# Attention logits from a pair of PSUM banks, and 512-column weight tiles in a two-block network on one Trainium2 core

## The chip, the cores and the metric

One core of one Trainium2 chip runs the whole kernel. The metric is the device time of one execution in microseconds. Three timed executions of the kernel before took 1380.38, 1381.72 and 1386.56 us, median 1381.72 us.

## The reference

Two networks run one after the other on 256 tokens of 1024 channels. Each has two layers. A layer of the first one normalises the stream, modulates it by the vector `c`, multiplies it by one wide matrix, runs three mixers of 8 heads of 64 channels, gates them and merges them:

```python
u = rms_norm(x, norm_g) * (1 + scale[:, None]) + shift[:, None]
z = u @ w_in
ya = dsa_attention(...)              # top-k by an index score, then softmax
yb = swa_sinks_attention(...)        # a window of 128 keys, with sinks
yc = stick_breaking_attention(...)
merged = sigmoid(ma) * (ya @ w_br_a) + sigmoid(mb) * (yb @ w_br_b) + sigmoid(mc) * (yc @ w_br_c)
x = x + gate[:, None] * (merged @ w_out)
```

A layer of the second network works on two streams of 256 tokens, a context and x. Its four mixers are HGRN2 (a gated linear scan, from context to x), grouped attention with normed queries and keys, differential attention (two softmax maps over 32 channels each; the second times lambda is subtracted), and window attention with a sink; 4 heads each. For x the attentions see 512 keys (context and x), for the context 256.

## The kernel before, in words

The streams are kept channel-major, as [128 channels, 8, 256 tokens]. **Large products.** Operands are float32 values that are split exactly into two float32r parts, high and low, and each product takes three matmuls for each 128 input channels: high by high, high by low, low by high. A weight tile has 256 columns. `raw` (L212) loads half of it, 512 rows and so 512 KB, by one DMA from SP's queue; `wtile` (L223) has `split` (L110) copy it to `wh` on ScalarE (L111) and subtract it to `wl` on VectorE (L112). There are three buffers for raw weights and four each for `wh` and `wl`. `proj_tok` (L248) makes a token-major result [128 tokens, 2 token tiles, up to 256 columns] in one PSUM bank: 128x128 pieces of the stream are loaded as TensorE's stationary operand, and the weights move past them, 256 columns a matmul; one token tile is computed to the end, then the other. `proj_ch` (L259) makes a channel-major result, with pieces of the weights stationary and 256 tokens moving. Token-major results that need rotary embedding go through `rope` on VectorE (L359, L370) and are transposed on TensorE by `tok_to_ch` (`T`, L108). All other matmuls are recorded under `mm`, L104. The index scores of block 1 have 324 columns, made as tiles of 256 and 68.

**PSUM.** The eight banks are four pools: `pj` 3 (projections), `lg` 2 (logits), `tr` 2 (transposes), `py` 1 (outputs of attention).

**Attention.** `probs` (L389) takes one bank of `lg`, holding the logits of one head (512 keys), two heads (256) or four (128). VectorE reduces the maximum from it (L397), ScalarE takes the exponentials and their row sums (L402); the bank is free when these are done. `weights_t` (L598) scales by the reciprocal (L610), transposes by TensorE, and copies the result to SBUF (L617); in `diff`, `p_times_v` (L405) does the last two (L412), behind the subtraction of the two maps (L931 to L933). Heads lie two to a 128-channel tile: even heads use rows 0 to 63 of TensorE's array, odd heads rows 64 to 127. In `gqa` (L883), `causal_softmax` (L620) and the index scores (L492) the bank of one row group is written with both its heads, or its one, then that of the other group. `diff` (L911) multiplies the queries by a mask to `qz` (L921), so that a product over all 128 rows sees only the 32 channels of one map. The levels of the scan `gla` (L753), and its first level `small`, issue all products of one row group to one bank, then those of the other group to the other.

**Order.** The program text gives the work; the Tile framework's scheduler then lays it out as one fixed order for each engine, by simulated times. Independent work (the gates' projections, the modulation products `ada`) is so placed between the steps of the softmax. At run time each engine takes its instructions in that order and waits at semaphores. The loop of `gqa` over the banks of logits reads (L890):

```python
for hs in ([[0, 2], [1, 3]] if nh == 2 else [[h] for h in range(4)]):
...
    e = self.probs(hs, L, logits, nm, ss, nsink)
    pt = self.weights_t(e, hs, L, nm, ss, sink)
```

Of the kernel before, what the change touches and what calls it, by code (L numbers as in the profile page):

```python
# [27 lines left out]
def _ap(t, base, dims):  # L28
# [5 lines left out]
       ("cs32", (2, 2, 32)), ("dmask", (4,)))  # L34
# [24 lines left out]
class Net:  # L59
    """Residual streams are kept channel-major, [128 channels, 8, 256 tokens].  Operands of the large products are  # L60
    float32 values split exactly into two float32r parts (high, low); a product takes high*high + high*low + low*high."""

    BUFS = {"th": 3, "pe": 3, "ro": 2, "rt2": 1, "pt": 3, "kc": 1, "gc": 1, "rstd": 1, "score": 1, "cs": 1, "rc": 1, "g1": 1, "g2": 1, "g4": 1}

    def __init__(self, ctx, tc, I):
# [11 lines left out]
        self.lg = pool("lg", 2, space=ps)  # L77
# [7 lines left out]
    # ---------------------------------------------------------------- tiles  # L85
# [9 lines left out]

    def halves(self, name, tags):
        """a [128, 8, 256] tile in two pieces"""
        return Halves([self.K(name, [128, 4, 256], tag=t) for t in tags])
# [15 lines left out]
    # ------------------------------------------------------------ constants  # L114
    def load_consts(self):
# [6 lines left out]
        self.mhalf = C.tile([128, 8], F32, name="mhalf")  # L122
# [20 lines left out]
    def more_consts(self):  # L143
# [34 lines left out]
        # -lambda of the differential attention, per layer  # L178
# [13 lines left out]
        # forget gate lower bounds -> f = A + B * tanh(z / 2)  # L192
# [18 lines left out]
    # -------------------------------------------------------------- weights  # L211
    def raw(self, ap, k0, c0, n, spare=False):  # L212
        """rows k0*128..(k0+4)*128, columns c0..c0+n"""
        if spare and self.spare:
            w = self.K("wsp", [128, 4, 256], tag=self.spare[self.nspare % len(self.spare)])
            self.nspare += 1
        else:
            w = self.wr.tile([128, 4, 256], F32, name="wr", tag="wr")
        self.nc.sync.dma_start(out=w[:, :, :n], in_=ap[k0 * 128:k0 * 128 + 512, c0:c0 + n].rearrange(  # L219
            "(k p) n -> p k n", p=128))  # L220
        return w

    def wtile(self, ap, c0, n=256, kt=8, pre=None):  # L223
        """columns c0..c0+n of ap [kt*128, N], split: w[part](k) -> [128, n]"""
        hs, ls = [], []
        for k in range(0, kt, 4):
# [1155 lines left out]
```

## Time and profile before

| | |
|---|---|
| time, median of 3 | 1381.72 us |
| profiled execution: span from first to last instruction | 1377.4 us |
| TensorE (PE) busy | 1330.4 us, 97% |
| weight loads of TensorE (PEld) busy | 1164.2 us, 85% |
| VectorE (DVE) busy | 844.3 us, 61% |
| ScalarE (ACT) busy | 655.1 us, 48% |
| mean granted TensorE clock | 0.986 |
| HBM traffic | 205.07 MB, mean 149 GB/s |

The profile comes from one execution with its own time. The page gives its span, 1377.4 us, 4.3 us below the median of the three timed runs; that difference is what lies around the span. In rows, names stand as out<-in: `ps` is any PSUM tile, `ps<-wh,uh` a product with `wh` moving past a piece of `uh`, or the other way round. A float32 matmul of the program shows as two records (two passes), so counts of attention matmuls in the trace are twice those of the program. Ends of matmuls are modelled, so the distance between starts is what tells how long one holds the array.

### The profile page before, as it was taken

Reading aid. Unit: us, or ns where it says so; the run is one execution under the profiler, and the core shown is the slowest. Engines: PE = TensorE matmul, PEld = TensorE weight load, DVE = VectorE, ACT = ScalarE, POOL = GpSimd, SP = SyncE. Lnnn points to the kernel's source line nnn. Section 1 sums busy time; section 2 is a strip of 40 time slices with the busy share of each in tenths; the row PEclk is TensorE's granted clock in tenths of the full one; section 3 lists DMA queues with packets and bytes.
Section 4 is the critical chain, followed back from the end, with each engine's and each line's share of the span. In section 5 each row is a group of like instructions: output and inputs, shape, how many; then the busy total and the mean of one; then the engine's idle time right before and its main releaser. Section 6 shows DMA issues by size and latency. Waiting matters only on the chain.

```text
span 1377.4 us, 27990 instructions
## 1 busy us (share of the span) xinstructions
PE 1330.4 (97%) x11682; PEld 1164.2 (85%) x11682; DVE 844.3 (61%) x1744; ACT 655.1 (48%) x1178; POOL 25.4 (2%) x23
## 2 busy tenths in 40 slices
PE   5999999999999999999998999999999998999996
PEld 2998987899889898789998989977877788997774
DVE  3795454655559544565576366756577777775764
ACT  3455555544444545654443233346455546534652
POOL 0000000000000000000000000000000000000000
PEclk9899999999999999999999999999999999999998
DMA  9754746568746474547764442322143355522111
GB/s 330 216 151 131 232 142 190 158 204 266 227 124 184 123 212 141 153 138 220 211 214 153 135 142 63 109 93 77 52 139 118 107 154 159 175 81 62 62 62 46
DMA packets 199214, 205.07 MB, mean 149 GB/s; under 512 B 8368, under 2 KB 197424, under 8 KB 198448
## 3 DMA queue, kind: packets, MB, share of 16 engines
q1 hardware_dynamic: 199088, 203.28, 48.3%
q8 instruction: 92, 1.51, 0.4%
q14 instruction: 34, 0.28, 0.1%
HBM read 199.06 MB, written 4.19 MB: 148 GB/s over the span
## 4 chain that ended last, share of the span: by engine, by line
PE 82%; DMA 6%; DVE 4%; issue 4%; ACT 2%; SPq 1%; POOL 0%; POOLq 0%; ACTq 0%; DVEq 0%
PE ps L104 77%; PE ps L108 5%; DMA wr<-w_in 4%; DMA wsp<-w_ada 2%; DVE wl L112 2%; ACT wh L111 1%; SPq L219 1%; DMA wr<-w_out 0%; DMA cT<-ctx 0%; DVE KTc L829 0%; DVE af L439 0%; ACT Xx L1305 0%; ACT pe L402 0%; ACT L566 0%; DVE QTc L827 0%
## 5 line engine op out<-in xcount | busy, mean ns | idle before, releaser
L112 DVE TENSOR_TENSOR wl<-wr,wh 128x1024 fp32r<-128x1024 f32 (+1 forms) x270 | 328.4, 1217 | 258.3 <-ACT wh L111 255.8
L111 ACT ACTIVATE wh<-wr 128x1024 fp32r<-128x1024 f32 (+1 forms) x270 | 284.6, 1055 | 378.2 <-PE ps L104 255.2
L104 PE MATMUL ps<-uh,wh 128*128 128x256 f32 x704 | 202.2, 287 | 2.4 <-ACT thm L566 2.4
L104 PE MATMUL ps<-ul,wh 128*128 128x256 f32 x704 | 200.9, 285 | 0.0
L104 PE MATMUL ps<-uh,wl 128*128 128x256 f32 x704 | 200.8, 285 | 0.0
L104 PEld LDWEIGHTS ps<-uh,wh 128*128 128x128 f32 x704 | 132.7, 188 | 8.2 <-issue 4.4
L104 PEld LDWEIGHTS ps<-ul,wh 128*128 128x128 f32 x704 | 132.8, 189 | 1.9 <-issue 1.7
L104 PEld LDWEIGHTS ps<-uh,wl 128*128 128x128 f32 x704 | 132.7, 188 | 1.9 <-issue 1.6
L104 PE MATMUL ps<-wh,uh 128*128 128x256 f32 (+1 forms) x416 | 120.2, 291 | 2.0 <-ACT uh L440 1.2
L104 PE MATMUL ps<-wl,uh 128*128 128x256 f32 (+1 forms) x416 | 119.9, 289 | 1.0 <-DVE wl L112 1.0
L104 PE MATMUL ps<-wh,ul 128*128 128x256 f32 (+1 forms) x416 | 120.0, 289 | 0.1
L402 ACT ACTIVATE pe<-ps,nm 128x512 f32<-128x512 f32 (+2 forms) x160 | 84.9, 539 | 54.4 <-DVE nm L397 41.1
L397 DVE TENSOR_REDUCE nm<-ps 128x1 f32<-128x512 f32 (+2 forms) x104 | 71.1, 687 | 42.2 <-PE ps L104 42.0
L104 PEld LDWEIGHTS ps<-wh,uh 128*128 128x128 f32 x416 | 81.2, 196 | 4.1 <-ACT uh L440 1.4
L104 PEld LDWEIGHTS ps<-wl,uh 128*128 128x128 f32 x416 | 81.3, 196 | 1.8 <-DVE wl L112 1.3
L104 PEld LDWEIGHTS ps<-wh,ul 128*128 128x128 f32 x416 | 81.5, 196 | 1.2 <-DVE ul L441 0.9
L104 PE MATMUL ps<-wh,hxh 128*128 128x256 f32 x256 | 72.4, 283 | 0.0
L104 PE MATMUL ps<-wh,hxl 128*128 128x256 f32 x256 | 72.1, 281 | 0.0
L104 PE MATMUL ps<-wl,hxh 128*128 128x256 f32 x256 | 72.0, 281 | 0.0
L104 PE MATMUL ps<-hxh,wh 128*128 128x256 f32 x224 | 64.9, 294 | 4.2 <-ACT hxh L440 4.2
L104 PE MATMUL ps<-hxl,wh 128*128 128x256 f32 x224 | 64.6, 290 | 2.7 <-DVE hxl L441 2.7
L104 PE MATMUL ps<-hxh,wl 128*128 128x256 f32 x224 | 64.6, 290 | 0.6 <-DVE wl L112 0.6
(351 smaller groups left out, 3150.7 us busy)
## 6 DMA issues: line engine op xcount, KB each, us to landing
wr<-w_in SPq DMA_DIRECT2D x204, 512.0 KB, 4.0
wsp<-w_ada SPq DMA_DIRECT2D x68, 512.0 KB, 5.7
wr<-w_out SPq DMA_DIRECT2D x40, 512.0 KB, 3.7
wr<-w_ada SPq DMA_DIRECT2D x28, 512.0 KB, 3.9
wr<-w_br_a SPq DMA_DIRECT2D x8, 512.0 KB, 3.9
wr<-w_br_c SPq DMA_DIRECT2D x8, 512.0 KB, 4.6
wr<-w_br_b SPq DMA_DIRECT2D x8, 512.0 KB, 4.6
Xx<-resx SPq DMA_DIRECT2D x2, 1024.0 KB, 4.7
```

The costliest lines, as they stand in the source:

```text
L104: self.nc.tensor.matmul(o, l, r, start=start, stop=stop, skip_group_check=True)
L108: self.nc.tensor.transpose(o, i, self.ident[:n, :n])
L111: self.nc.scalar.activation(h, x, AF.Copy)
L112: self.nc.vector.tensor_tensor(l, x, h, op=OP.subtract)
L219: self.nc.sync.dma_start(out=w[:, :, :n], in_=ap[k0 * 128:k0 * 128 + 512, c0:c0 + n].rearrange("(k p) n -> p k n", p=128))
L397: nc.vector.tensor_reduce(nmx, p, axis=AX.X, op=OP.max, negate=True)
L402: nc.scalar.activation(e[:, j, :], p[:, j, :], AF.Exp, bias=nm[:, h:h + 1], accum_out=ss[:, h:h + 1])
```

## The change

**Logits.** The pool `lg` holds one tile of two banks, `pp`, in place of two single banks. The new `banks` issues the logits alternately: a product of row group 0 to the first bank, one of row group 1 to the second, and so on. This is used in `causal_softmax` and `gqa`, and written out for the index scores and in `gla`. The tile is one buffer: the next pair of logits waits until the last reader of both banks is done. `diff` drops the mask product; the queries and keys of its two maps are now operands of 32 rows, one bank for each map, with 512 keys as with 256. With 256 keys, the maximum is now taken by two reductions of 256 columns in place of one of 512.

**Projections.** A weight tile of more than 256 columns is loaded in chunks of two 128-row groups of 512 columns: the same 512 KB, in rows of 2 KB in place of 1 KB. The products go through a chunk for both token tiles before the next chunk; a wide token-major projection has two banks of `pj`, one for each token tile. The 324 columns of the index scores are one tile. In block 1, `idx`, `aq`, `ak`, `av`, `cv` and `bq` are wide; in block 2 queries, keys and values of mixer B, queries and keys of C, values of C with queries of D. `rope` runs for each token tile by itself (`rope_1`). `proj_ch` keeps 256 columns.

In numbers of the program, matmuls fall from 9935 to 8879. 2544 token-major products of 256 columns become 528, and 960 of 512 columns; 96 of 256 and 96 of 68 columns become 96 of 324. VectorE has 1693 instructions in place of 1714, ScalarE 1047 in place of 1020.

```diff
-        self.lg = pool("lg", 2, space=ps)
+        self.lg = pool("lg", 1, space=ps)
...
+    def P2(self, *shape):
+        t = self.lg.tile([128, 2, 512], F32, name="pp")
...
+    def load_rows(self, w, ap, k0, c0):
+        _, kc, n = w.shape
+        self.nc.sync.dma_start(out=w, in_=ap[k0 * 128:(k0 + kc) * 128, c0:c0 + n].rearrange("(k p) n -> p k n", p=128))
+    def wtile(self, ap, c0, n=256, kt=8, pre=()):
+        kc = 2 if n > 256 else 4
+        ws = []
+        for c, k in enumerate(range(0, kt, kc)):
+            r = pre[c] if c < len(pre) else self.raw(ap, k, c0, n)
+            h = self.wh.tile([128, kc, 1024 // kc], F32R, name="wh", tag="wh")
+            l = self.wl.tile([128, kc, 1024 // kc], F32R, name="wl", tag="wl")
             self.split(h[:, :, :n], l[:, :, :n], r[:, :, :n])
+            ws.append((k, kc, h[:, :, :n], l[:, :, :n]))
+        return ws
...
+    def proj_tok(self, w, u):
+        n = w[0][2].shape[-1]
+        if n <= 256:
+            bank = self.P(self.pj, [128, 2, 256])
+            ps = [bank[:, t, :n] for t in range(2)]
+        else:
+            ps = [self.P(self.pj, [128, 512])[:, :n] for _ in range(2)]
+        for k0, kc, *hl in w:
+            for t, p in enumerate(ps):
+                ts = slice(t * 128, t * 128 + 128)
+                for k in range(kc):
+                    for i, (a, b) in enumerate(self.TERMS):
+                        self.mm(p, u[a][:, k0 + k, ts], hl[b][:, k], start=k0 + k == i == 0 and (t == 0 or n > 256),
+                                stop=k0 + k == 7 and i == 2)
+        return ps if n > 256 else bank[:, :, :n]
...
+    def banks(self, nh, L, q, k, mask=None):
+        ps = self.P2(nh, L)
+        for j in range(nh):
+            for a, p in enumerate(ps):
+                self.mm(p[:, j, :], q(a, j), k(a, j), start=j == 0, stop=mask is None)
+        if mask is not None:
+            for p in ps:
+                o, m = mask(p)
+                self.mm(o, self.identb, m, start=False, stop=True)
+        return ps
...
+        def wide(nm, n=512):
+            ps = self.proj_tok(self.wtile(wi, OFF1[nm], n, pre=pre.get(nm, ())), u)
+            self.after_tile()
+            self.after_tile()
+            return [(p, t, slice(128 * t, 128 * t + 128)) for t, p in enumerate(ps)]
+        def qk_1(nm, dst, sc):
+            for p, t, ts in wide(nm):
+                ro = self.W("ro", [128, 8, 64])
+                self.rope_1(ro, p, 8, self.cs1[:, t])
+                self.tile_to_ch(ro.rearrange("p h d -> p (h d)"), [(dst[:, :, ts], sc)])
...
-        w = self.wtile(wi, OFF1["idx"], pre=pre.get("idx"))
...
-        w = self.wtile(wi, OFF1["idx"] + 256, 68, pre=pre.get("iw"))
...
+        for p, t, ts in wide("idx", 324):
...
-        for nm, dst, i, sc in (("aq", aqT, 1, 0.125), ("ak", akT, 0, 1.0), ("ak", akT, 1, 1.0)):
-            qk_a(self.wtile(wi, OFF1[nm] + 256 * i), dst[:, 2 * i:2 * i + 2], sc)
...
+        qk_1("aq", aqT, 0.125)
+        qk_1("ak", akT, 1.0)
...
+            for cs in ([[0, 1]] if nh == 2 else [[0], [1]]):
+                ps = self.banks(nh, L, lambda a, j: qT[64 * a:64 * a + 64, cs[j], t * 128:t * 128 + 128],
+                                lambda a, j: kT[64 * a:64 * a + 64, cs[j], k0:k0 + L], mask)
+                for a in range(2):
+                    hs = [2 * c + a for c in cs]
+                    e = self.probs(hs, L, ps[a], nm, ss, nsink)
+                    pt = self.weights_t(e, hs, L, nm, ss, sink)
...
-                qz = self.W("qz", [128, 2, 128])
                 ct = h // 2
-                mo = 2 * (h % 2)
-                V.tensor_tensor(qz, qT[:, ct:ct + 1, t * 128:t * 128 + 128].to_broadcast([128, 2, 128]),
-                                self.dmask[:, mo:mo + 2, None].to_broadcast([128, 2, 128]), op=OP.mult)
-                es = []
-                for ms in ([[0], [1]] if L == 512 else [[0, 1]]):
-                    def logits(p):
-                        for j, m in enumerate(ms):
-                            self.mm(p[:, j, :], qz[:, m], kT[:, ct, k0:k0 + L])
-                    e = self.probs([2 * h + m for m in ms], L, logits, nm, ss)
-                    es += [e[:, j, :] for j in range(len(ms))]
+                rows = [slice(64 * (h % 2) + 32 * m, 64 * (h % 2) + 32 * m + 32) for m in range(2)]
+                ps = self.banks(1, L, lambda m, j: qT[rows[m], ct, t * 128:t * 128 + 128],
+                                lambda m, j: kT[rows[m], ct, k0:k0 + L])
+                es = [self.probs([2 * h + m], L, ps[m], nm, ss)[:, 0] for m in range(2)]
...
         def small(lhs, rh, first, mask):
-            for a in range(2):
-                p = self.P(self.lg, [128, 2, 2, 32])
-                for ct in range(2):
-                    for t in range(2):
+            ps = self.P2(2, 2, 32)
+            for ct in range(2):
+                for t in range(2):
+                    for a in range(2):
                         for j in range(4):
                             t0 = 128 * t + 32 * j
-                            self.mm(p[32 * j:32 * j + 32, ct, t, :], lhs[64 * a:64 * a + 64, ct, t0:t0 + 32],
+                            self.mm(ps[a][32 * j:32 * j + 32, ct, t, :], lhs[64 * a:64 * a + 64, ct, t0:t0 + 32],
                                     rh(2 * ct + a, t0))
+            for a, p in enumerate(ps):
...
+                streams(self.wtile(wi, 1024, 512), ss, qkv_b)
...
+                streams(self.wtile(wi, 1792, 512), ss, kv_c)
...
+            streams(self.wtile(wi, 1536, 512), ss, qk_c)
...
+            streams(self.wtile(wi, 2048, 512), ss, vc_qd)
```

How the instructions stand on TensorE and ScalarE, at two places. First TensorE, the differential attention of the context in layer 0 of block 2 (`kC` keys, `pe` exponentials, `pt` transposed weights, `vC` values; xN counts the program's instructions). Before:

```order
L104 MATMUL ps_10857<-kC_9941,qz_10855 128x256 x2
L104 MATMUL ps_10877<-kC_9941,qz_10875 128x256 x2
L108 MATMUL ps_10825<-ident_111,pe_10818 128x128 x2
L104 MATMUL ps_10768<-vC_10072,pt_10788 128x64 x2
L104 MATMUL ps_10768<-vC_10072,pt_10808 128x64 x2
L108 MATMUL ps_10845<-ident_111,pe_10838 128x128 x2
L104 MATMUL ps_10897<-kC_9941,qz_10895 128x256 x2
```

Now:

```order
L118 MATMUL pp_9886<-kC_9067,qC_9069 128x256 x2
L122 MATMUL ps_9879<-ident_111,pe_9870 128x128 x2
L118 MATMUL ps_9862<-vC_9068,pt_9882 128x64 x2
L118 MATMUL pp_9906<-kC_9067,qC_9069 128x256 x2
L122 MATMUL ps_9899<-ident_111,pe_9890 128x128 x2
L118 MATMUL ps_9862<-vC_9068,pt_9902 128x64 x2
L118 MATMUL pp_9926<-kC_9067,qC_9069 128x256 x2
```

Before, the logits of two heads stand next to each other ahead of the transposes of an earlier one. Now each head's logits stand behind the values' product of the head before the last, and all eight heads follow this pattern of three groups, with nothing else between.

Second, ScalarE at the differential attention of x in layer 1 (L459 the exponentials of the first, then the second map, L469 the copy of the transposed weights of the head before), now:

```order
L459 ACTIVATE pe_13537,ss_13508<-pp_13533,nm_13507 128x512
L469 ACTIVATE pt_13527<-ps_13522 128x512
L459 ACTIVATE pe_13540,ss_13508<-pp_13533,nm_13507 128x512
L459 ACTIVATE pe_13561,ss_13508<-pp_13557,nm_13507 128x512
L469 ACTIVATE pt_13551<-ps_13546 128x512
L459 ACTIVATE pe_13564,ss_13508<-pp_13557,nm_13507 128x512
```

and TensorE at the same place:

```order
L118 MATMUL pp_13557<-kC_12229,qC_13020 128x512 x2
L122 MATMUL ps_13546<-ident_111,pe_13537 128x128 x4
L118 MATMUL ps_13505<-vC_12230,pt_13551 128x64 x4
L118 MATMUL pp_13581<-kC_12229,qC_13020 128x512 x2
L122 MATMUL ps_13570<-ident_111,pe_13561 128x128 x4
L118 MATMUL ps_13505<-vC_12230,pt_13575 128x64 x4
```

The copy for one head stands between the two exponentials of the next, and the values' product of one head before the next pair of logits; here too nothing else is between.

## Rows read from the trace of the kernel before

**Rows 1.** The page: engines' busy time, granted clock in 40 slices, chain by engine.

```profile
PE 1330.4 (97%) x11682; PEld 1164.2 (85%) x11682; DVE 844.3 (61%) x1744; ACT 655.1 (48%) x1178; POOL 25.4 (2%) x23
...
PEclk9899999999999999999999999999999999999998
...
PE 82%; DMA 6%; DVE 4%; issue 4%; ACT 2%; SPq 1%; POOL 0%; POOLq 0%; ACTq 0%; DVEq 0%
```

**Rows 2.** Chain of waits, one piece in order of time: start, us, what.

```profile
617.10 29.60 PE ps L104 x256
```

**Rows 3.** Windows: stretch, us, PE, PEld, DVE, ACT, POOL busy (instructions), clock, DMA, GB/s.

```profile
25.00:30.00 5.00, 3.05 (x36) 1.06 (x36) 2.71 (x9) 1.96 (x5) 0.00 (x0) 1.00 1.10 349
30.00:35.00 5.00, 2.79 (x20) 0.99 (x12) 2.12 (x10) 1.92 (x4) 0.00 (x0) 0.60 1.09 350
55.00:60.00 5.00, 5.00 (x31) 5.00 (x31) 3.34 (x6) 1.80 (x4) 0.00 (x0) 0.67 0.69 183
400.00:405.00 5.00, 5.00 (x24) 5.00 (x25) 1.38 (x3) 2.18 (x3) 0.00 (x0) 0.50 0.49 132
405.00:410.00 5.00, 5.00 (x39) 5.00 (x38) 2.04 (x5) 0.98 (x2) 0.00 (x0) 0.85 0.67 203
1300.00:1320.00 20.00, 19.87 (x109) 12.75 (x110) 16.17 (x54) 12.75 (x36) 1.81 (x1) 1.00 0.01 2
```

**Rows 4.** Timeline of TensorE in the 68-column tile of layer 0: start, us, operation.

```profile
54.77 0.28 PE L104 MATMUL ps<-wl,uh 128*128 128x68 f32 x1
54.88 0.39 PE L104 MATMUL ps<-wh,uh 128*128 128x68 f32 x1
55.08 0.41 PE L104 MATMUL ps<-wh,ul 128*128 128x68 f32 x1
55.29 0.41 PE L104 MATMUL ps<-wl,uh 128*128 128x68 f32 x1
```

**Rows 5.** The same view, index scores of layer 0, four heads.

```profile
67.27 1.14 PE L104 MATMUL ps<-iqT 64*128 64x256 f32 x8
68.34 0.38 PE L104 MATMUL ps<-wh,uh 128*128 128x256 f32 x1
```

**Rows 6.** The same view, window attention of x, layer 1, two heads.

```profile
1305.17 1.12 PE L104 MATMUL ps<-kD,qD 64*128 64x512 f32 x2
1306.22 0.23 PE L104 MATMUL ps<-c_bandm,c_identb 128*128 128x128 bf16 x1
1306.29 0.61 PE L108 MATMUL ps<-ident,pe 128*128 128x128 f32 x4
1306.83 1.12 PE L104 MATMUL ps<-kD,qD 64*128 64x512 f32 x2
```

**Rows 7.** The same view, differential attention of x, layer 1.

```profile
1295.66 1.88 PE L104 MATMUL ps<-kC,qz 128*128 128x512 f32 x4
1297.38 1.00 PE L104 MATMUL ps<-vC,pt 128*128 128x64 f32 x8
1298.28 1.12 PE L104 MATMUL ps<-kC,qz 128*128 128x512 f32 x2
```

**Rows 8.** The same view, one level of the context's scan.

```profile
845.27 1.68 PE L104 MATMUL ps<-QTc,KTc 64*128 64x128 f32 x16 [0.20 <-DVE QTc L827]
```

**Rows 9.** Groups of VectorE by line and form: count, busy, mean ns, idle before.

```profile
L397 DVE TENSOR_REDUCE nm<-ps 128x1 f32<-128x512 f32 x64 | 43.8, 687 | 25.0 <-PE ps L104 24.9
...
L829 DVE TENSOR_TENSOR KTc<-KTc,FTc 128x512 f32<-128x512 f32 x16 | 11.0, 690 | 0.8
```

**Rows 10.** The same for ScalarE: exponentials and copies of the weights.

```profile
L402 ACT ACTIVATE pe<-ps,nm 128x512 f32<-128x512 f32 x64 | 43.9, 686 | 41.5 <-DVE nm L397 29.3 <-DVE nm L399 5.9 <-PE ps L108 2.1
...
L402 ACT ACTIVATE pe<-ps,nm 128x256 f32<-128x256 f32 x64 | 29.8, 473 | 9.5 <-DVE nm L397 8.5 <-DVE nm L399 0.6
...
L412 ACT ACTIVATE pt<-ps 128x512 f32<-128x512 f32 x16 | 9.5, 594 | 2.3 <-PE ps L108 2.3
...
L412 ACT ACTIVATE pt<-ps 128x256 f32<-128x256 f32 x8 | 3.1, 384 | 1.4 <-PE ps L108 1.1
```

More of the change, by code (lines that the diff above doesn't have):

```diff
@@ L94, in P @@
         return pool.tile(shape, dt, name="ps")
+    def P2(self, *shape):
+        t = self.lg.tile([128, 2, 512], F32, name="pp")
+        n = math.prod(shape)
+        out = []
+        for a in range(2):
+            v = t[:, a, :n]
+            if len(shape) == 2:
+                v = v.rearrange("p (a b) -> p a b", a=shape[0])
+            elif len(shape) == 3:
+                v = v.rearrange("p (a b c) -> p a b c", a=shape[0], b=shape[1])
+            out.append(v)
+        return out
     def halves(self, name, tags):
@@ L363, in rope @@
             sw = lambda a, t: a[:, t].rearrange("p (h b a d) -> p h b a d", h=H, b=nb, a=2)
-            for t in range(2):
+            for t in range(nt):
                 V.tensor_tensor(sw(t2, t), sw(src, t)[:, :, :, ::-1],
@@ L379, in rope, with rope_1, tile_to_ch @@
             V.tensor_tensor(dst, t1, b, op=OP.add)
+    def rope_1(self, dst, src, H, cs, **k):
+        self.rope(dst[:, None], src[:, None], H, cs[:, None], **k)
+    def tile_to_ch(self, src, outs):
+        n = src.shape[-1] // 128
+        p = self.P(self.tr, [128, 4, 128])
+        for j in range(n):
+            self.T(p[:, j], src[:, 128 * j:128 * j + 128])
+        j = 0
+        for dst, scale in outs:
+            m = dst.shape[1]
+            self.nc.scalar.activation(dst, p[:, j:j + m], AF.Copy, scale=scale)
+            j += m
     def tok_to_ch(self, dst, src, scale=1.0, n=2):
@@ L535, in block1 @@
         cv = self.K("cv", [128, 2, 512], tag="a6")
-        for i, w in tiles("cv", 2):
-            A.activation(cv[:, :, 256 * i:256 * i + 256], self.proj_tok(w, 256, u), AF.Copy)
+        for p, t, _ in wide("cv"):
+            A.activation(cv[:, t], p, AF.Copy)
         gate("c")
@@ L798, in gla @@
             elif out:
-                for a in range(2):
-                    p = self.P(self.lg, [128, 2, 2, 128])
-                    for ct in range(2):
-                        for t in range(2):
+                ps = self.P2(2, 2, 128)
+                for ct in range(2):
+                    for t in range(2):
+                        for a, p in enumerate(ps):
                             h = 2 * ct + a
@@ L1361, in _constants @@
     out["gmask64"] = top(p ^ q, 64).astype(f)
-    out["dmask"] = np.where(p // 32 == np.arange(4)[None], 32 ** -0.5, 0).astype(f)
     pack = lambda names: np.ascontiguousarray(np.concatenate([out[n].reshape(128, -1) for n in names], 1))
```

321 lines of the change are left out of this document (149 added, 172 removed).

## The prediction

> **What bounds the kernel now.** I read the page first. PE is busy for 97% of the span, at a granted clock of 0.9 or more in all slices but the second and the last; the chain that ended last lies on PE for 82% [rows 1]. DVE and ACT have 61% and 48%. So a microsecond of PE work taken away is a microsecond won, as long as PE finds something else to do. The chain of waits then shows what this is like in a stage of weights: 256 matmuls in 29.60 us with no wait, 115.6 ns each [rows 2]. The stages of attention are as dense: the window attention of the last layer has PE busy for 19.87 of 20 us, although DVE is busy for 16.17 and ACT for 12.75 there [rows 3]. This last row is the warning: PE has work there because independent work stands between the softmax steps, and DVE and ACT have not much to spare.
>
> The windows also show where the clock is low. It is 0.67 in 55 to 60 us, 0.50 in 400 to 405 and 0.85 in 405 to 410, with PE busy all the time [rows 3]. The timeline shows what PE did before the first of these: products of 68 columns, 111 ns apart, and then 200 to 210 ns apart, the lower level of 1.2 GHz [rows 4].
>
> **The change, part by part: PE work taken off.**
>
> *Wide projections.* 1920 products of 256 columns become 960 of 512. Two of the old ones take 2 x 115.6 = 231 ns. No row has a float32r product of 512 columns. A float32 pass of 512 columns takes 430 ns (four in 1.72 us [rows 7]), two cycles for each column at 2.4 GHz, and 115.6 ns is a little over one cycle for each of 256; so the new one lies between 215, half of that pass, and 231, no gain. I take 218, near the pass, which has its fixed part hidden: 960 x 13.2 = 12.7 us (0 to 15.5).
>
> *Index scores.* 96 x (115.6 + 111) ns = 21.8 us [rows 2, 4] become 96 products of 324 columns. Between 136 (half of 430, by columns) and 146 (115.6 by columns), I take 140: 13.4 us. Gain 8.4 us (7.7 to 8.7).
>
> *Heads of two row groups.* A head of 512 keys takes 1.05 us, from 1305.17 to 1306.22 [rows 6]; the same number of columns is in a bank with two heads of 256 or four of 128. In the index scores eight passes of 256 columns, from both row groups, took 1.07 us, from 67.27 to 68.34 [rows 5]: as much as one group alone would. So a pair side by side costs what one costs now. There are 32 pairs (16 of 512 keys, 12 of 256, 4 of 128): 32 x 1.05 = 33.6 us.
>
> *Differential attention.* Both maps take 1.72 us with 512 keys [rows 7]. In 32-row groups I take 1.05, as for 64-row groups side by side: 16 x 0.67 = 10.7 us; with 256 keys half of both, 8 x 0.33 = 2.6 us. No row shows 32 rows. If they don't overlap, four passes cost 2.10, and the term is -7.6 instead of 13.3; if they stream like full rows, 0.86, it is 17.9. I take 13.3, from the nearest rows [rows 5, 6]. The 24 mask products that go from DVE have no one waiting for DVE's total, and count nothing.
>
> *Scan.* Nine groups like the one of 1.68 us [rows 8] should lose some 0.7 each: 6.4 us. But PE waited 0.20 us there for DVE's product (L827) of the next level, which takes no less now. DVE's products of 0.69 us a level [rows 9] set the pace, so all of it comes back as waiting: net 0 (up to 6.4).
>
> *Clock.* The 68-column products go, and with them, I think, the three low stretches: 5 x 0.33 + 5 x 0.50 + 5 x 0.15 = 4.9 us [rows 3]. If other work brings the clock down at the same place, 0.
>
> Sum: 12.7 + 8.4 + 33.6 + 13.3 + 4.9 = 72.9 us (the scan left out on both sides).
>
> A rule that speaks against the third and fourth terms: the Trainium skill ("TensorE: Matmul & The Clock Gate", Part 3, Packing small matmuls) says that matmuls start and end strictly in program order, with only weight loads pulled ahead. By it, of the two passes that each product has, only the second of one head could run beside the first of the next, and the two terms would shrink to about 20 us together; but the index scores were issued group by group, both heads of one before the other, and still took 1.07 us for eight passes [rows 5], so this trace disagrees.
>
> **What is given back.** The pair of banks is one buffer. The next logits wait until the exponential of the second map or head is done; before, one bank of two was free earlier. Where other work stands between, this costs nothing. By the order on PE there is none at the context's differential attention (8 heads), the last 3 heads of x's in layer 0, 7 of 8 in layer 1, four pairs of window attention in layer 0, one in layer 1 and two of mixer B in layer 1.
>
> *Context, 8 heads.* Logits 0.53; maximum of the first map 0.4 (an estimate: 256 of 512 columns of 687 ns [rows 9]); exponentials 0.47 each, with the copy of the transposed weights, 0.38, between them [rows 10]; 0.6 for row sums and hand-overs (an estimate). Cycle 2.9 us. PE's own work is 0.53 + 0.27 + 0.45 = 1.25 (half of the transposes' 0.54 [rows 6] and of the values' product, 0.90 from 1297.38 to 1298.28 [rows 7]). Idle: 8 x 1.65 = 13.2 us.
>
> *x, 10 heads.* Logits 1.05, hand-over 0.15, reduction 0.69, exponential 0.69, copy 0.59 [rows 9, 10]; the values' product that waits for this copy, 0.90, stands before the next logits, and the second exponential ends at about the same time. Cycle 4.2 us; PE's work 1.05 + 0.54 + 0.90 = 2.5. Idle: 10 x 1.7 = 17 us.
>
> *Window attention and mixer B, 7 pairs.* The same chain with the scaling by the reciprocal, 0.5 more, is 4.7 us; PE has logits 1.05, masks 0.14, two times the transposes 0.54 and two products of about 0.5: 3.3. Idle: 7 x 1.4 = 9.8 us.
>
> *Two of three projection banks.* A wide product needs both; the first is read by DVE while the second token tile is still being computed (six products of 218 ns), and rotary embedding of a tile is two or three operations of some 0.69 us [rows 9]. Other projections in the third bank cover this: 0. If that cover is gone, 0.5 us for each of 22 wide products, 11 us.
>
> Given back: 13.2 + 17 + 9.8 = 40 us. Loads stay 512 KB each. Net 72.9 - 40 = 32.9 us, so the span goes from 1377.4 to 1344.5. The median of the runs is 4.3 us above the span; with this I predict **1349 us** (own range 1333 to 1366).
>
> **The rivals.**
>
> *Gaps filled.* The hand-overs are shorter, or two heads' steps interleave better than my chain. Half of the idle time is 1349 - 20 = 1329; none is 1309. For: the chain of waits lies on ACT for only 2% today. Against: the order has nothing to put there. Chance 0.18 (1309 to 1333).
>
> *The pair costs everywhere.* In the 31 filled ones too (25 pairs and 6 heads of `diff`), the reductions and exponentials stand behind weight splits on DVE and ACT, and one buffer can't hide it; each gives back its gain, 25 x 1.05 + 6 x 0.67 = 30 us: 1379; with the 11 us of the projection banks 1390. For: DVE's 16.17 of 20 us [rows 3]. Against: in these stretches the order puts several us of projections between. Chance 0.12; no change.
>
> *Rows overlap less, or wide products gain nothing.* By program order, the third term keeps half and the fourth a fifth: 27 us less, 1376. This is the rule of the Trainium skill named above. The same by rows, if 32-row groups don't overlap (20.9) and 512 columns gain nothing (12.7): 1383. For: no row shows either. Against: [rows 5, 7]. Chance 0.06, of it 0.02 for the strict order; no change.
>
> *The clock falls (slower).* PE was busy for 3.05 of 5 us in 25 to 30 us, and the clock fell to 1.2 GHz in the next stretch, 0.60 [rows 3]. My unfilled heads leave PE with a like share or less: 1.25 of 2.9 and 2.5 of 4.2. If it falls there, logits and values' products on the chain take twice as long (1.05 + 0.90 more for a head of x): 8 x 0.7 + 10 x 2.0 + 7 x 2.1 = 40 us, and each of two stretches ends with some us at the lower clock among weights, 2.5 to 3.3 lost as at 400 to 410 us: 1349 + 45 = **1394**. It decides when all three kinds fall; the context's heads alone cost 6 us and stay in my range. For: the clock at 30 and at 55 us [rows 3]. Against: at 25 to 30 us itself the clock still was 1.00. Chance 0.12.
>
> **How the numbers follow.** My forecast has 0.52. Half a per cent, 6.9 us, is about what a measurement of this kernel can tell: faster is under 1374.8, slower over 1388.6. Faster: 0.52 + 0.18 and 0.04 from the lower edges of the second and third rivals, 0.74. Slower: the clock, 0.11 of its 0.12, and 0.01 from the second rival's upper end, 0.12. The rest, 0.14, is no change. The range leaves out the lower half of the filled gaps (0.09) and the cases above 1388 (0.12), so about 2 in 10: 1318 to 1388.
>
> **What would show it.** Right: wide products 218 ns apart; pairs of logits at 1.05 us for 512 keys; full clock at the index scores; about 4.2 us from logits to logits in x's differential attention, with PE's idle time put down to ACT's exponentials and copies, and PE's share of the span near 94%. Wrong: logits pairs near 2 us, 512 columns at 231, a granted clock under 1 in the attention stages, or idle time of PE before wide products put down to DVE's rotary embedding.

## The result and the profile after

The changed kernel takes 1455.91 us (median of three, 1453.94 to 1457.92) against 1381.72: a ratio of 1.054, 95% interval 1.052 to 1.056. It is slower by 74 us, where I predicted 1349. Its profiled execution has a span of 1452.0 us.

The page of the changed kernel, the lines that answer to [rows 1]:

```profile
PE 1333.9 (92%) x10626; PEld 1113.0 (77%) x10626; DVE 842.5 (58%) x1723; ACT 670.0 (46%) x1205; POOL 24.0 (2%) x20
...
PEclk8999998999999999999999979996996999998598
...
PE 82%; ACT 6%; DVE 5%; DMA 4%; issue 1%; SPq 1%; POOL 0%; POOLq 0%; ACTq 0%; DVEq 0%
```

PE has 1056 fewer records and is busy as long as before. Three numbers explain this, and the table below has them for every kernel of this study. "Low" is the time in which PE is busy while the granted clock is at its lower level, 1.2 GHz. "Work" is PE's busy time less half of that, an estimate of the busy time it would have at 2.4 GHz. "Idle" is the time in which no matmul runs. The three are worked out from the instructions and the clock in each trace. Span = work + low / 2 + idle.

| kernel (profiled execution) | span | work | low | idle | median of runs |
|---|---|---|---|---|---|
| before | 1377.4 | 1316.5 | 27.8 | 47.0 | 1381.7 |
| after | 1452.0 | 1256.0 | 155.8 | 118.1 | 1455.9 |
| e1 wide tiles only | 1380.7 | 1304.1 | 45.0 | 54.0 | 1385.5 |
| e2 paired logits only | 1456.8 | 1268.4 | 154.5 | 111.2 | 1457.3 |
| e3 after, two single banks | 1418.5 | 1296.2 | 132.1 | 56.3 | 1420.9 |
| e7 as e3, masked queries | 1378.2 | 1294.1 | 45.4 | 61.4 | 1380.6 |
| e9 after, masked queries | 1464.1 | 1267.8 | 149.0 | 121.7 | 1463.0 |
| e13 before, 32-row operands | 1421.2 | 1323.1 | 108.6 | 43.8 | 1422.7 |
| e10 after, two pairs | 1417.5 | 1255.6 | 147.5 | 88.1 | 1408.9 |
| e11 same pools, one pair | 1475.3 | 1257.0 | 165.2 | 135.7 | 1476.7 |
| e4 after, extra full-row work | 1461.8 | 1277.4 | 138.3 | 115.3 | 1464.6 |
| e6 before, 324-column tile | 1362.4 | 1306.7 | 17.8 | 46.8 | 1368.6 |
| e8 as e6, all row groups alternate | 1363.3 | 1295.3 | 37.9 | 49.1 | 1361.2 |
| e12 as e6, scan alternates | 1358.6 | 1300.2 | 28.3 | 44.3 | 1362.0 |

From before to after the work falls by 60.5 us, the low clock costs 64.0 more, and idle time grows by 71.1: together +74.6, the change of the span.

The same sums by stretch show where it lies. A stretch goes from the first product of its stage to the last: the stick-breaking attention in each layer of the first network, the scans in each layer of the second, and from each end of a scan to the last value product of the window attention, which holds the three attention mixers and what the order lays between them.

| stretch | low before | low after | idle before | idle after |
|---|---|---|---|---|
| attention of the second network | 0 | 93.7 | 4.0 | 45.3 |
| stick-breaking attention | 0 | 16.9 | 2.4 | 20.8 |
| scans | 0 | 13.6 | 1.4 | 14.6 |
| all the rest | 27.8 | 31.6 | 39.2 | 37.4 |

It is also seen in the windows of the changed kernel (stretch, us, PE, PEld, DVE, ACT, POOL busy, clock, DMA, GB/s), which answer to [rows 3]: the stick-breaking attention of the first layer, the differential attention of the context, and that of x in the last layer.

```profile
200.00:220.00 20.00, 15.11 (x95) 13.53 (x92) 5.39 (x6) 12.06 (x13) 0.00 (x0) 0.83 0.27 81
220.00:240.00 20.00, 13.17 (x69) 7.60 (x69) 4.37 (x7) 10.26 (x15) 0.00 (x0) 0.66 0.33 105
...
980.00:1000.00 20.00, 15.62 (x54) 9.25 (x54) 9.16 (x28) 7.04 (x26) 0.00 (x0) 0.50 0.00 0
...
1340.00:1360.00 20.00, 15.82 (x52) 9.45 (x51) 8.33 (x17) 7.63 (x19) 0.00 (x0) 0.50 0.00 0
```

No engine is full in them: ACT and DVE are busy for less than half of each of the last two, PE for 78 and 79%, at half speed.

The timeline of PE shows the cycle (start, us, operation, idle before and its releaser). First the context's heads:

```profile
970.54 0.70 PE L118 MATMUL pp<-kC,qC 32*128 32x256 f32 x4 [0.42 <-ACT pe L459]
971.60 0.41 PE L122 MATMUL ps<-ident,pe 128*128 128x128 f32 x2 [0.36 <-DVE pe L978]
972.54 0.66 PE L118 MATMUL ps<-vC,pt 128*128 128x64 f32 x4 [0.53 <-ACT pt L469]
974.06 1.22 PE L118 MATMUL pp<-kC,qC 32*128 32x256 f32 x4 [0.85 <-ACT pe L459]
...
976.37 1.11 PE L118 MATMUL ps<-vC,pt 128*128 128x64 f32 x4 [0.47 <-ACT pt L469]
977.88 1.22 PE L118 MATMUL pp<-kC,qC 32*128 32x256 f32 x4 [0.40 <-ACT pe L459]
```

From logits to logits it is 3.52 us at full clock and then 3.82 at half; I had estimated 2.9. The heads of x in the last layer:

```profile
1332.22 1.13 PE L118 MATMUL pp<-kC,qC 32*128 32x512 f32 x4
1333.28 0.66 PE L122 MATMUL ps<-ident,pe 128*128 128x128 f32 x4
1335.44 1.81 PE L118 MATMUL ps<-vC,pt 128*128 128x64 f32 x8 [1.51 <-ACT pt L469]
1337.18 2.08 PE L118 MATMUL pp<-kC,qC 32*128 32x512 f32 x4
1339.19 1.12 PE L122 MATMUL ps<-ident,pe 128*128 128x128 f32 x4
1341.35 1.97 PE L118 MATMUL ps<-vC,pt 128*128 128x64 f32 x8 [1.04 <-ACT pt L469]
1343.25 2.08 PE L118 MATMUL pp<-kC,qC 32*128 32x512 f32 x4
```

Four passes of 32 rows take 1.06 us at full clock (1332.22 to 1333.28), so the maps do run side by side; at half clock 2.01. The cycle goes from 4.96 us to 6.07. The first of the two is not all at full clock: its values' product already takes 1.74 us, where such a product took 0.90 before [rows 7], so at full clock the cycle would be some 4.1 us (an estimate), about what I had added up. Each wait is for ACT's copy of the transposed weights, which stands behind the exponentials.

PE's waits in the changed kernel (waited for: us in total, times, longest) name the same places:

```profile
PE ps L118 <- ACT pt L469: 15.7, 20, 1.5
PE ps L118 <- ACT thm L622: 14.5, 6, 4.9
PE ps L122 <- DVE pe L666: 9.6, 8, 2.6
...
PE pp L118 <- DVE QTc L880: 5.4, 2, 4.8
PE pp L118 <- DVE stx L729: 5.0, 1, 5.0
```

`stx` belongs to the stick-breaking attention, where I expected nothing. `thm` is the tanh of the merge's gates: the order puts their projections into the same stretch, and all six waits for it lie there, the longest 4.89 us at 211.10. From its first to its last logits this attention takes 48.1 us before (165.4 to 213.5) and 81.8 after (143.7 to 225.5), and the second layer's is the same. Most of that is other work laid between; lost are 18.4 us of idle time and 8.4 us by the clock, in both layers together. The wide products are the other surprise. At full clock they are 233 ns apart, just two of the old ones:

```profile
62.97 0.40 PE L118 MATMUL ps<-wl,uh 128*128 128x512 f32 x1
63.21 0.39 PE L118 MATMUL ps<-wh,uh 128*128 128x512 f32 x1
63.44 0.40 PE L118 MATMUL ps<-wh,ul 128*128 128x512 f32 x1
```

### The profile page after: what moved, and what is told of

Its sections match the earlier page's. It is cut to its first block, busy times and chain, and to the rows that moved or that the text cites. A ratio compares the mean times of both kernels' runs of the same rounds, so it can differ in the third digit from the quotient of the medians.

```text
span 1452.0 us, 25877 instructions
## 1 busy us (share of the span) xinstructions
PE 1333.9 (92%) x10626; PEld 1113.0 (77%) x10626; DVE 842.5 (58%) x1723; ACT 670.0 (46%) x1205; POOL 24.0 (2%) x20
## 4 chain that ended last, share of the span: by engine, by line
PE 82%; ACT 6%; DVE 5%; DMA 4%; issue 1%; SPq 1%; POOL 0%; POOLq 0%; ACTq 0%; DVEq 0%
PE ps L118 68%; PE pp L118 10%; PE ps L122 5%; ACT pe L459 2%; DMA wr<-w_in 1%; DVE nm L454 1%; ACT wh L125 1%; SPq L239 1%; DVE wl L126 1%; DMA wsp<-w_ada 1%; ACT pt L469 1%; DMA wr<-w_ada 1%; DMA wr<-w_out 1%; DMA cT<-ctx 0%; ACT pt L673 0%
## 5 line engine op out<-in xcount | busy, mean ns | idle before, releaser
L459 ACT ACTIVATE pe<-pp,nm 128x512 f32<-128x512 f32 (+2 forms) x160 | 85.0, 536 | 85.7 <-DVE nm L454 64.9
L454 DVE TENSOR_REDUCE nm<-pp 128x1 f32<-128x512 f32 (+3 forms) x112 | 72.7, 649 | 80.2 <-PE pp L118 46.9
L118 PE MATMUL ps<-wh,uh 128*128 128x512 f32 (+2 forms) x224 | 84.6, 382 | 1.7 <-ACT uh L497 1.4
L118 PE MATMUL ps<-wh,ul 128*128 128x512 f32 (+2 forms) x224 | 84.2, 378 | 0.0
L118 PE MATMUL ps<-wl,uh 128*128 128x512 f32 (+2 forms) x224 | 82.9, 377 | 0.0
L122 PE MATMUL ps<-ident,pe 128*128 128x128 f32 x336 | 65.5, 312 | 10.2 <-DVE pe L666 9.6
L122 PEld LDWEIGHTS ps<-ident,pe 128*128 128x128 f32 x336 | 42.8, 157 | 36.8 <-issue 32.2
L673 ACT ACTIVATE pt<-ps 128x512 f32<-128x512 f32 x64 | 38.0, 596 | 49.1 <-PE ps L122 49.0
L118 PE MATMUL ps<-wsp,cs 128*32 128x256 f32 x560 | 48.0, 424 | 11.6 <-DMA wsp<-w_ada 9.4
L118 PE MATMUL ps<-wh,hxh 128*128 128x512 f32 (+1 forms) x160 | 56.3, 352 | 0.0
L118 PE MATMUL ps<-wl,hxh 128*128 128x512 f32 (+1 forms) x160 | 56.2, 351 | 0.0
```

What stands on the lines that cost most here:

```text
L118: self.nc.tensor.matmul(o, l, r, start=start, stop=stop, skip_group_check=True)
L122: self.nc.tensor.transpose(o, i, self.ident[:n, :n])
L454: nc.vector.tensor_reduce(nmx, p, axis=AX.X, op=OP.max, negate=True)
L459: nc.scalar.activation(e[:, j, :], p[:, j, :], AF.Exp, bias=nm[:, h:h + 1], accum_out=ss[:, h:h + 1])
L673: nc.scalar.activation(pt[:, :nb], p[:, :nb], AF.Copy)
```

## The experiments

All variants are scheduled anew, so each has an order of its own; ratios are to the kernel before, run beside them (1380.87, 1380.14 and 1379.82 us), with 95% intervals.

**Halves of the change: e1, e2, e6, e3.** My theory at this point: the paired logits cause the loss (P). The rival: the wide tiles have a good part in it (W).

e1 puts the logits of before into the changed kernel:

```diff
-        self.lg = pool("lg", 1, space=ps)
+        self.lg = pool("lg", 2, space=ps)
...
-    def banks(self, nh, L, q, k, mask=None):
...
+        p = self.P(self.lg, [128, nh, L])
+        logits(p)
```

> The changed kernel with the logits of before: two single banks, one row group after the other, the mask product in the differential attention. Theory P (the loss comes from the paired logits): in the changed kernel products of 512 columns are 233 ns apart, twice the 115.6 ns of 256 columns, so they gain nothing; the 324-column index scores gain some 8 us and the clock at the 68-column tiles 5 us: 1368 us, 1360 to 1380. Theory W (the wide products, which hold two of three projection banks, cause a good part of the loss): 1400 us or more.

e2 is the other half, the new logits in the kernel before:

```diff
-        self.lg = pool("lg", 2, space=ps)
+        self.lg = pool("lg", 1, space=ps)
...
+    def banks(self, nh, L, q, k, mask=None):
```

> The kernel before with the paired logits alone, all projections as before. Theory P: the loss of the whole change and the 13 us of the index scores besides: about 1468 us, 1440 to 1480, with the clock at 1.2 GHz in the differential attention as in the changed kernel. Theory W: 1400 us or less.

e6 has the one tile of 324 columns and nothing else that is wide:

```diff
-        w = self.wtile(wi, OFF1["idx"], pre=pre.get("idx"))
...
-        w = self.wtile(wi, OFF1["idx"] + 256, 68, pre=pre.get("iw"))
...
+        ps = self.proj_tok(self.wtile(wi, OFF1["idx"], 324, pre=pre.get("idx", ())), u)
```

> The kernel before with the index scores as one tile of 324 columns and weight chunks used up for both token tiles; all other tiles stay at 256 columns, logits as before. If products of 512 columns gain nothing: 1368 us, 1362 to 1376, the same as the run with all wide tiles within 5 us, with no spell of low clock at the index scores of either layer. If 512 columns do gain, this run is slower than that one by 8 us or more.

Measured: e2 1457.33 us (1.054, 1.051 to 1.056), all of the loss. e6 1368.63 (0.990, 0.987 to 0.992), the time expected; but a low spell is left at the start of the second layer's index tile (0.57 from 376 to 380 us). e1 1385.46 (1.003, 1.002 to 1.004), above what P gave and below what W gave, and 17 us from e6, where I had expected 5 at most. The 512-column tiles, with the order that they bring, gain nothing over e6 and cost these 17 us. In the table low clock is up by 27.2 us, which costs 13.6, and idle time is up by 7.2. Most of it lies at the scans: 20.2 us of low clock against 0, idle time 7.9 against 0.8. A wait of e1 at the end of the context's scan, and its windows there:

```profile
828.57 0.64 PE L118 MATMUL ps<-wr,cs 128*32 128x256 f32 x8 [2.72 <-DMA wr<-w_ada]
```

```profile
830.00:840.00 10.00, 6.27 (x35) 5.63 (x34) 9.10 (x13) 4.64 (x5) 0.00 (x0) 0.50 0.66 208
840.00:850.00 10.00, 10.00 (x80) 9.59 (x79) 1.98 (x4) 2.67 (x5) 0.00 (x0) 0.50 0.28 87
```

and of e6 at the same levels:

```profile
820.00:830.00 10.00, 10.00 (x88) 9.49 (x87) 8.30 (x17) 2.06 (x3) 0.00 (x0) 1.00 0.20 60
830.00:840.00 10.00, 10.00 (x95) 9.60 (x94) 2.44 (x5) 3.21 (x6) 0.00 (x0) 1.00 0.15 49
```

In e1, PE has waited 2.72 us for weights of the modulation product `ada`; then the clock is at 0.50, with DVE busy for 9.10 of 10 us at the scan's last levels and PE for 6.27. In e6 the order has projections there, and the clock stays up. Every kernel with wide tiles in this study has a spell of 17 to 24 us at the end of this scan, none without them has it. So P stands for the sign, and W for 17 us.

e3 keeps the alternating text, but each bank is a buffer of its own:

```diff
-        t = self.lg.tile([128, 2, 512], F32, name="pp")
...
-            v = t[:, a, :n]
+            v = self.P(self.lg, [128, 512])[:, :n]
```

> The changed kernel with the two banks of a pair as two buffers of one bank, each free by itself; products are written in the program in the same alternating order. If it is the pair as one buffer that leaves TensorE without work: 1370 to 1400 us, TensorE idle for 40 to 70 us instead of 118. If less work of TensorE lays the chains of VectorE and ScalarE bare whatever the buffers are: over 1430 us. If the scheduler now pulls the two products of a pair apart, the logits take their old time (two times 1.05 us) again.

Measured: 1420.88 (1.028, 1.026 to 1.030), between what the two theories gave. Idle falls from 118.1 to 56.3 us as expected of the one buffer, and the scheduler did pull pairs apart (work 40 us up). But the time stays 35 us above e1, and not by idle time: low clock is 132.1. The windows of e3 at the last differential attention:

```profile
1300.00:1320.00 20.00, 19.79 (x100) 11.47 (x100) 11.24 (x23) 10.67 (x26) 0.00 (x0) 0.79 0.09 27
1320.00:1340.00 20.00, 19.46 (x53) 10.53 (x52) 9.11 (x21) 7.28 (x18) 0.00 (x0) 0.50 0.00 0
```

The clock falls in the first window, with PE busy for 19.79 of 20 us, and in the second it stays at 1.2 GHz with PE busy for 19.46. There are no gaps to speak of. That gave a new theory (R): products of 32 rows bring the clock down by themselves. Its rival (I): the waits do.

**32 rows or waits: e7, e9, e13, e4.** e7 and e9 put the masked queries back, 128 rows for each map, into e3 and into the changed kernel:

```diff
-                rows = [slice(64 * (h % 2) + 32 * m, 64 * (h % 2) + 32 * m + 32) for m in range(2)]
-                ps = self.banks(1, L, lambda m, j: qT[rows[m], ct, t * 128:t * 128 + 128],
-                                lambda m, j: kT[rows[m], ct, k0:k0 + L])
+                qz = self.W("qz", [128, 2, 128])
...
+                ps = self.banks(1, L, lambda m, j: qz[:, m], lambda m, j: kT[:, ct, k0:k0 + L])
```

> The run with two single banks, with the masked queries of before in the differential attention (128 rows, one map after the other) in place of operands of 32 rows; the rest as there. In that run PE was busy for 47.2 of the 47.8 us of low clock at the differential attention of x in layer 1. Theory R (it is the 32-row products themselves that bring the clock down, not idle time): the low spell there goes, and the time falls from 1421 to 1385 to 1395 us. Rival I (the clock falls because PE waits in short gaps): the spell stays, 1415 to 1430 us.

> The changed kernel, pair of banks and all, with the masked queries in the differential attention. Theory R: PE has 13 us more work there, but the clock stays up: the spell of 41 us in layer 1 goes, 1425 to 1440 us. Rival I: PE waits as long as before for the pair, the clock falls all the same, and the longer logits come on top: 1456 to 1475 us.

e13 does the opposite in the kernel before, and nothing else:

```diff
-                            self.mm(p[:, j, :], qz[:, m], kT[:, ct, k0:k0 + L])
+                        self.mm(p[:, 0, :], qT[rw, ct, t * 128:t * 128 + 128], kT[rw, ct, k0:k0 + L])
```

> The kernel before with operands of 32 rows in the differential attention, each map from a single bank, and nothing else changed. Theory R (32-row products bring the clock down where PE is not otherwise loaded): a spell of low clock of 20 us or more with PE busy in it, at the differential attention of x in layer 1, 1390 to 1420 us. Rival: only less work, 1370 to 1383 us and no such spell.

Measured: e7 1380.57 (1.000, 0.999 to 1.001), 4 us below R's range: 40 us less than e3 with about the same work and 5 us more idle; low clock falls from 132.1 to 45.4. e13 1422.73 (1.030, 1.028 to 1.033), a little over the range: 43 us more than before from this alone, with idle 3 us less and low clock up by 81 us, which costs 40. A window of e7 and two of e13, from the last heads of the differential attention into the window attention behind it:

```profile
1290.00:1310.00 20.00, 19.72 (x96) 11.49 (x95) 16.01 (x44) 12.56 (x33) 0.00 (x0) 1.00 0.00 0
```

```profile
1320.00:1330.00 10.00, 9.57 (x52) 5.89 (x50) 6.89 (x12) 6.09 (x12) 0.00 (x0) 0.97 0.32 106
1330.00:1350.00 20.00, 20.00 (x53) 10.57 (x52) 7.72 (x24) 5.99 (x17) 0.00 (x0) 0.50 0.00 1
```

Both have PE busy all the time; one is at 1.00, the other at 0.50. With single banks R is shown, in both directions, with a limit: from 1290 to 1320 us e13 has 32-row logits with projections between them, and the clock is 1.00. It falls where nothing but transposes and values' products stands between, and stays low through the window attention, whose logits have 64 rows. With the pair R is not enough: e9 is at 1462.99 (1.060, 1.058 to 1.062), slower than the changed kernel and in rival I's range. PE in e9:

```profile
1344.74 3.44 PE L118 MATMUL pp<-kC,qz 128*128 128x512 f32 x4 [1.10 <-ACT pe L459]
1347.98 0.88 PE L122 MATMUL ps<-ident,pe 128*128 128x128 f32 x4
1349.54 1.10 PE L118 MATMUL ps<-vC,pt 128*128 128x64 f32 x8 [0.69 <-ACT pt L469]
1351.75 3.62 PE L118 MATMUL pp<-kC,qz 128*128 128x512 f32 x4 [1.10 <-ACT pe L459]
```

The cycle is 7.01 us with 128 rows; in this stage the clock now goes up and down between heads instead of staying low, but PE waits twice a head, the longer time at L459, the exponentials that hold the pair. At the context's heads the clock stays low as before: 0.50 from 980 to 1000 us, with PE busy for 16.51 of 20.

e4 adds work to the changed kernel:

```diff
+                spare = self.P(self.pj, [128, 512])
+                self.mm(spare[:, :L], self.ident, es[0])
```

> The changed kernel with one more product a head in the differential attention, that nothing reads: 128 rows, 256 or 512 columns of the first map's exponentials, 0.43 or 0.86 us at full clock, in the time in which PE waits for the second map. 17 us of useless work. If full-row work there holds the clock: the cycle of x in layer 1 goes from 6.07 us back to some 5.0, and the time falls by 5 to 25 us, to 1431 to 1451. If the clock falls whatever is put there: 1456 to 1470 us.

Measured: 1464.55 (1.060, 1.058 to 1.063), by the total as if it did nothing for the clock. But the stage that I had named tells the other thing. PE in e4, differential attention of x, last layer:

```profile
1355.17 1.13 PE L118 MATMUL pp<-kC,qC 32*128 32x512 f32 x4
1356.23 0.66 PE L122 MATMUL ps<-ident,pe 128*128 128x128 f32 x4
1357.90 1.13 PE L118 MATMUL ps<-pe,ident 128*128 128x512 f32 x2 [1.02 <-ACT pe L459]
1358.87 1.00 PE L118 MATMUL ps<-vC,pt 128*128 128x64 f32 x8
1359.80 1.13 PE L118 MATMUL pp<-kC,qC 32*128 32x512 f32 x4
```

and its window there:

```profile
1350.00:1360.00 10.00, 7.85 (x39) 4.34 (x40) 5.48 (x14) 4.58 (x12) 0.00 (x0) 1.00 0.00 0
```

The cycle is 4.63 us, against 6.07, at full clock, with about the same share of busy time as the changed kernel has at half clock. So full-row work held the clock in this stage. In the attention of the second network low clock falls from 93.7 to 54.4 us, which gives back 19.6; but the table has 21.4 us more work, and the new order adds a low spell of 23.9 us at the end of x's scan in the last layer that the changed kernel doesn't have. The total of this run decides nothing.

**One buffer: e10, e11.** To test the buffer itself, two pools that differ in it alone; both have two banks for projections and one for transposes:

```diff
-        self.pj = pool("pj", 3, space=ps)
-        self.lg = pool("lg", 1, space=ps)
-        self.tr = pool("tr", 2, space=ps)
+        self.pj = pool("pj", 2, space=ps)
+        self.lg = pool("lg", 2, space=ps)
+        self.tr = pool("tr", 1, space=ps)
```

> The changed kernel with two buffers for the pair of logits banks (four banks), two banks for projections and one for transposes. To be compared with the next run, which has the same pools but one pair. Theory B (one buffer for the pair is what leaves PE without work): PE idle at least 25 us less and at least 30 us faster than the next run. Rival: the softmax chains of VectorE and ScalarE set the pace also with two pairs, less than 10 us between the two.

> The same pools, two banks for projections and one for transposes, and one buffer for the pair; two banks stay unused. Slower than the changed kernel by what the missing projection and transpose banks cost: 1460 to 1540 us. It is the reference for the run with two pairs.

Measured: e10 1408.88 (1.022, 1.017 to 1.027), e11 1476.73 (1.069, 1.067 to 1.072): 68 us from the second pair. In the table, where e10's execution is the longest of its four (1419.25 us), the work is the same, idle time is 47.6 us less and low clock 17.7, which costs 8.9. At the stick-breaking attention e11 has 20.3 us of idle time and 23.5 of low clock, e10 none of either. e10 is 47 us faster than the changed kernel too, though it has fewer banks for everything else. The one buffer is shown to be the largest single cause; the rest that e10 has over the kernel before, 29 us, comes with 147.5 us of low clock. No run has two pairs and masked queries.

**What is worth keeping: e8, e12.** e8 is e6 with logits of two row groups alternating from two single banks in all but the differential attention; e12 has that in the scan alone:

```diff
-                for a in range(2):
-                    p = self.P(self.lg, [128, 2, 2, 128])
-                    for ct in range(2):
-                        for t in range(2):
+                ps = self.P2(2, 2, 128)
+                for ct in range(2):
+                    for t in range(2):
+                        for a, p in enumerate(ps):
```

> The kernel before with the 324-column index tile (1368.6 us), and besides that logits of two row groups issued alternately from two single banks in the window, top-k and grouped attention and in the scan; the differential attention keeps its masked queries and its one bank for two maps of 256 keys. If row groups side by side are worth their 1.05 us a pair where the order has other work: 1345 to 1362 us. If VectorE and ScalarE bound these stages anyway: 1364 to 1374 us. If the alternating order costs as in the run with two single banks and narrow rows: over 1380 us.

> The 324-column index tile (1368.6 us) with the alternating issue from two single banks in the scan alone. The same in all attentions and the scan gave 1361.2 us. If VectorE sets the pace of the scan: 1365 to 1371 us, and the 7 us come from the attentions. If they come from the scan: 1360 to 1364 us.

Measured: e8 1361.20 (0.986, 0.984 to 0.988), e12 1361.99 (0.987, 0.985 to 0.989). Both beat both kernels, by 1.3 to 1.4%, and the scan alone gives what all of them give. Over e6 it is a small gain: 6.6 us by the medians, 4 to 5 by the ratios, whose intervals touch; the work in the table falls by 6.5. A group of the scan in e6, then in e12:

```profile
827.34 1.71 PE L124 MATMUL ps<-QTc,kc 64*128 64x128 f32 x16
```

```profile
826.70 1.16 PE L137 MATMUL ps<-QTc,kc 64*128 64x128 f32 x16
```

Side by side the group takes 0.55 us less, and with single banks this is kept.

## Why the prediction was wrong

I forecast a span of 1344.5 us and it is 1452.0. Of the 107.5 us between them, 68.9 are the clock: I credited 4.9 us and it cost 64.0. Idle time makes 24.7 (46.4 forecast with the scan's 6.4, 71.1 measured) and work 13.9 (74.4 forecast to go, the scan included, 60.5 gone). The step that failed is so the sum's clock: it took every attention stage at 2.4 GHz, and a fall was only a rival. The second is the list of places where PE waits for the pair, which lacked the stick-breaking attention.

*Wide projections* (12.7 us): failed. My lower bound was half of a float32 pass; the row shows the upper one, 233 ns, no gain. They also were not free: 17 us (e1 against e6). I had asked only whether a projection bank comes free in time, and not what else the larger tiles displace in the order.

*Index scores* (8.4): right. In e6 the products of 324 columns are 147 ns apart, a little over my 146, and the kernel is 12 us faster, where this term and the next make 13.3. *Clock at the 68-column tiles* (4.9): right in e6, where the low spells at 55 and 400 us are gone and low clock falls by 10.0 us. In the changed kernel it gained nothing: outside the three stages of the table low clock is 31.6 us against 27.8, and from 384 to 390 us, at the second layer's 324-column tile, its clock is 0.50.

*Heads of two row groups* (33.6) and *differential attention* (13.3): right as PE work; logits side by side take 1.06 us. With the wide term at nothing, my terms of work, the scan's 6.4 included, make 61.7 us; the table has 60.5. The Trainium skill's rule ("TensorE: Matmul & The Clock Gate", Part 3) of strict program order fits neither place in this trace: of the index scores, which stand group by group in PE's order, the first products of the two groups start 0.01 us apart (67.27 and 67.28) and alternating gains nothing (1.07 us before [rows 5], 1.06 after), and in the scan's group of [rows 8] the second row group starts 0.53 us behind the first, ahead of the first one's last three passes. In the scan alternating does gain 0.55 us; why the second group starts late is not shown.

*What is given back* (40, and 6.4 in the scan): in the stages that I listed the size was about right, in part by luck. In the attention of the second network idle time grew by 41.3 us. A head at the lower clock leaves less idle time than I had put (0.40 and 0.47 us at the context's, where I had 1.65; 1.05 at x's, where I had 1.7), and waits outside my list made up for it. The context's cycle, 3.5 us where I had 2.9, was too short. What the step had wrong is the list: I looked for heads with nothing between in the softmax mixers alone, although the stick-breaking attention holds the pair through two exponentials, a logarithm and two products. It lost 18.4 us of idle time and 8.4 by the clock. That is the pair's doing and not the wide tiles': its idle time is 19.5 us with the pair alone (e2), 5.0 with the wide tiles alone (e1) and none with two pairs (e10). The scans lost 13.2 us of idle time, where I had 6.4, and 6.8 by the clock.

*The clock* was my rival for the slower side, at 0.12 and 1394 us. Its place was right, and there its size too: I priced 40 us at the three kinds of heads and 5 at their ends, and the attention of the second network lost 46.9. What it lacked is the other 17 us of the 64, above all at the stick-breaking attention and the scans. The chance was too low, and the reason only half right. I argued from PE's share of busy time; e3 and e13 show the clock low with PE busy throughout, where logits of 32 rows stand without projections between. The masked queries, which I took for 10.7 us of waste, had been holding the clock. No rival reached 1455.91 us: the slowest stood at 1394.

*The pair costs everywhere* (0.12) was not borne out: in the first network's two softmax mixers PE is idle for 0.3 us at most, before and after. Of *rows overlap less, or wide products gain nothing* (0.06) the second half came true; rows do overlap. Two of the signs that I had named for being wrong were seen, 512 columns at 231 ns or more and a granted clock under 1 in the attention stages. Two sums in the prediction are a little off, the full-stream case of the differential attention (17.2, not 17.9) and the listed steps of x's cycle (4.1 us, not 4.2); neither moves the forecast by more than 1.3 us.

That the low clock follows from the pair's waits and not only from 32 rows is supported by e9, where it falls with full rows. In the attention of the second network low clock is 93.7 us in the changed kernel, 83.1 with masked queries alone (e9), 80.7 with single banks alone (e3) and 3.4 with both (e7): either cause is enough, and the two don't add up. From the changed kernel to e3 the time falls by 35 us and from there to e7 by 40, which is the whole loss.

## What to carry to other kernels

PE work saved in a stage is worth what the stage's chain of VectorE and ScalarE lets through: write down that chain with the buffer that it holds, for every stage that uses the buffer, and count two buffers before crediting two products side by side. Making PE's operands smaller, in rows or in columns, can cost the clock, which then taxes all work around it; look at the granted clock of the stage, not only at the share of busy time. Take parts of a change apart before judging it: here 324 columns and the scan's alternation gained 18 us (e12), and the changed kernel as a whole is 94 us slower than that.

## What I had not expected of the hardware

The granted clock fell to 1.2 GHz with PE all but fully busy. In e13 PE is busy for 9.57 of the 10 us around the fall and for 20.00 of the 20 after it; the products there are logits of 32 rows, then of 64, with transposes and values' products between. In the kernel before it fell among products of 68 columns, with PE busy for 5.00 of 5 us [rows 3, 4]. With 128-row logits in the differential attention and the same busy share it stayed at 2.4 GHz (e7). Float32r products cost 115.6 ns for 256 columns, 147 for 324 and 233 for 512, while a float32 pass of 512 columns and 128 rows takes 430: by the column, the float32r product is a little slower than half of it.
